# Two of four weight sums of a hybrid decoder layer, made by adding DMA transfers instead of VectorE

## The chip, the cores and the metric

The kernel runs on one core of one Trainium2 chip. A core has five engines with a queue of instructions each: TensorE (PE: matmuls, PEld: its weight loads), VectorE (DVE), ScalarE (ACT), GpSimd (POOL) and SyncE (SP). SP only issues transfers here, POOL issues some too. Transfers are carried out by 16 DMA engines. An engine takes its own instructions strictly in order, and engines wait for each other through semaphores.

The metric is the device time of one execution in microseconds, the median of several runs. One further execution is profiled; its span, from the first to the last instruction, is a little shorter than the time of a run.

## The reference, cut to what matters

One layer on x of 512 tokens by 1024 features, all in fp32: a SwiGLU feed-forward network (FFN 1, hidden width 2816), then a mixer that merges windowed attention with a gated linear recurrence, then a second SwiGLU (FFN 2), each with a norm before and after.

```
def swiglu(x, w_gate, w_up, w_down):
    return (jax.nn.silu(x @ w_gate) * (x @ w_up)) @ w_down
...
f = swiglu(rms_norm(h, ffn1_norm_pre[l]), ffn1_w_gate[l], ffn1_w_up[l], ffn1_w_down[l])
h = h + 0.5 * rms_norm(f, ffn1_norm_post[l])
u = rms_norm(h, mix_norm_pre[l])
proj = u @ w_in[l]
q, k, v, xr, yr, gl = jnp.split(proj, splits, axis=-1)
...
gates = jax.nn.sigmoid(gl).reshape(B, S, N_BRANCHES, D_MODEL)
merged = gates[:, :, 0] * attn_d + gates[:, :, 1] * rec_d
h = h + rms_norm(merged @ w_out[l], mix_norm_post[l])
f = swiglu(rms_norm(h, ffn2_norm_pre[l]), ffn2_w_gate[l], ffn2_w_up[l], ffn2_w_down[l])
h = h + 0.5 * rms_norm(f, ffn2_norm_post[l])
```

What matters for the change are the products of x with blocks of weights: `w_gate` and `w_up`, the q and k columns of `w_in`, and half of its gate columns `gl`. Attention has twelve heads in three groups; one head of each group is merged with the other two into one output head, so there are four rounds, each of three q and three k blocks.

## The kernel before, in words

**Exactness.** Every fp32 operand of a matmul is split into a high part of reduced precision (ACT, L266) and the rest (DVE, L267). A product is then three matmuls: high by high, high by low, low by high.

**The weight stream.** All weights lie in one DRAM array in the order of their use, in groups of up to 1 MB (128 rows by 2048 numbers). `raw_of` (L204 to L222) loads the next group into one of two buffers `raw` by a transfer on SP (L212). A buffer is free for the next load when the last reader of its weights is through.

**Seven-product pairs.** A pair is two blocks of 1024 by 128 weights, called u and g (for FFN up and gate, for attention k and q). Each is cut in two along the 1024 (`u0`, `u1`, `g0`, `g1`, each 128 rows by 512 numbers in `raw`), and the tokens are cut in two halves. Two by two by two blocks need eight products; by Winograd's form of Strassen's scheme seven are enough, for sums of weights and sums of tokens formed before. `w_forms` (L561 to L578) makes the weights for the seven products:

- `s12[:, 1] = u0 + u1` (L567), `s12[:, 0] = s12[:, 1] + g0` (L568), `u0 += g0` in place (L569), `g1 += s12[:, 0]` in place (L572): four adds on DVE of 128 by 512.
- Four splits: a from `g0`, `g1` as loaded (L571, for p1 and p2); b from `s12` (L573, for p6 and p5); c from `u0 + g0` and `u1` (L574, for p7 and p4); d from the new `g1` (L575, for p3).

`seven` (L580 to L619) runs the products in the order p1, p2, p6, p5, p7, p4, p3. Each is 12 matmuls of 256 columns (L591, L592, L593 in turn), 84 for a pair. Partial sums are copied out by ACT (L598) and added by DVE (L603).

There are 51 pairs: 17 in FFN 1 (hidden blocks 5 to 21), 16 in the mixer (twelve q and k pairs, named by block numbers such as (8,20), then four pairs of gate columns), and 18 in FFN 2. In the FFNs a "down" block, 48 matmuls of 512 columns against `w_down`, mostly follows every two pairs. In the mixer one round of attention (`attend`, L856 to L964) is written between the three pairs of the next round (`qk`, L835).

**Buffers.** Two of `raw`, two of `s12` (tag "s"), four of the large splits (a, b and c), two of d, five PSUM banks `acc` and three `aux`.

**The order.** A scheduler fixes the order of each engine's instructions when the program is built. Work is written in the order of the code; what stands under `tc.high_priority(offset=n)` is placed as if written n instructions earlier. `w_forms` stands under AHEAD = 100 and the evacuations of PSUM in `seven` under EVAC = 200. In the mixer `pair_of` (L828) makes the weight forms of the next pair ahead of the products of the present one, and the FFN's "prep" does the same.

**Attention's exchange.** `exchange` (L906 to L916) moves statistics across partitions: DVE masks them (L909), PE multiplies them by a constant matrix (L912), DVE masks and sums the result (L914, L916). It is called twice a round, and between the calls stand nine small operations (L919 to L931). PE takes L912 in its order among the products of the next round's pairs.

Of the kernel before, what the change touches and what calls it, by code (L numbers as in the profile page):

```python
# [13 lines left out]
ALU = mybir.AluOpType  # L14
AX = mybir.AxisListType

P = 128
# [136 lines left out]
def hybrid_layer(ctx: ExitStack, tc: tile.TileContext, xT: bass.AP, xN: bass.AP, wst: bass.AP,  # L154
                 first: bass.AP, rows: bass.AP, consts: bass.AP, bias: bass.AP, out: bass.AP):
    nc = tc.nc
    DVE, ACT, PE = nc.vector, nc.scalar, nc.tensor
# [44 lines left out]
    state = {"g": 0, "i": 0, "off": 0, "raw": None}  # L202

    def raw_of(key):  # L204

        g, i = state["g"], state["i"]
        grp = groups[g]
        if i == 0:
            w = grp[-1][1] + grp[-1][2]
            raw = wpool.tile([P, RAW_W], F32, name="raw", tag="raw", bufs=2)  # L210
            src = bass.AP(tensor=wst.tensor, offset=wst.offset + state["off"], ap=[[w, P], [1, w]])
            nc.sync.dma_start(raw[:, :w], src)  # L212
            state["raw"] = raw
            state["off"] += w * P
        k, o, w = grp[i]
        assert k == key, (k, key)
        src = state["raw"][:, o:o + w]
        if i + 1 == len(grp):
            state["g"], state["i"] = g + 1, 0
        else:  # L220
            state["i"] = i + 1
        return src  # L222

    def fetch(key, slot=None, ahead=0):

        with tc.high_priority(offset=ahead if slot else AHEAD):
            src = raw_of(key)
            w = src.shape[-1]
            t = slot() if slot else w8() if w > 512 else w4()
            split(t[:, 0, :w], t[:, 1, :w], src)  # L230
            return t[:, 0, :w], t[:, 1, :w]

    def w8():
        return wpool.tile([P, 2, 1024], F32R, name="w8", tag="w8", bufs=4)

    def w4():
        return wpool.tile([P, 2, 512], F32R, name="w4", tag="w4", bufs=2)
# [27 lines left out]
    def split(dh, dl, src):  # L265
        ACT.activation(dh, src, AF.Copy)  # L266
        DVE.tensor_sub(dl, src, dh.bitcast(F32))  # L267
# [293 lines left out]
    def w_forms(key):  # L561

        with tc.high_priority(offset=AHEAD):
            raw = raw_of(key)
            u0, u1, g0, g1 = (raw[:, i * 512:(i + 1) * 512] for i in range(4))
            s12 = spool[0].tile([P, 2, 512], F32, name="s12", tag="s", bufs=2)
            DVE.tensor_add(s12[:, 1, :], u0, u1)  # L567
            DVE.tensor_add(s12[:, 0, :], s12[:, 1, :], g0)  # L568
            DVE.tensor_add(u0, u0, g0)  # L569
            a, b, c, d = w8(), w8(), w8(), w4()  # L570
            split(a[:, 0, :], a[:, 1, :], raw[:, 1024:2048])  # L571
            DVE.tensor_add(g1, s12[:, 0, :], g1)  # L572
            split(b[:, 0, :], b[:, 1, :], s12.rearrange("p s c -> p (s c)"))  # L573
            split(c[:, 0, :], c[:, 1, :], raw[:, 0:1024])  # L574
            split(d[:, 0, :], d[:, 1, :], g1)  # L575
            lo, hi = slice(0, 512), slice(512, 1024)
            return {"p1": a[:, :, lo], "p2": a[:, :, hi], "p6": b[:, :, lo], "p5": b[:, :, hi],
                    "p7": c[:, :, lo], "p4": c[:, :, hi], "p3": d}  # L578
# [42 lines left out]
    def ffn(n, x, r, forms_x, apool, pss):  # L621
# [52 lines left out]
        for ev in ffn_order(n):  # L674
            if ev[0] == "std":
                j = ev[1]
                while len(pss) < 2 * j + 2:
                    pss.append(acc_ps())
                    gemm(pss[-1], fetch(keys[len(pss) - 1]), x)
                std_out(pss[2 * j], pss[2 * j + 1], j)  # L680
                if j < len(steps):
                    steps[j]()
            elif ev[0] == "prep":
                forms[ev[1]] = w_forms(("gu", n, ev[1]))
            elif ev[0] == "down":
                down(ev[1], ev[2])
            else:
                prod(ev[1], forms.pop(ev[1]), ev[2], ev[3])
# [4 lines left out]
    def act_two(pool):  # L693

        ts = [pool.tile([P, 8, T], F32R, name="act", tag="act", bufs=3) for _ in range(2)]
        return Act([ts[0][:, k, :] for k in range(8)], [ts[1][:, k, :] for k in range(8)])
# [22 lines left out]
    u1 = act_two(ap1)  # L719
# [9 lines left out]
    for k in range(KC):  # L729
        wh, wl, raw = wts[k]  # L730
# [30 lines left out]
    with ExitStack() as mx:  # L761
# [61 lines left out]
        pairs = [[(g * 4 + hd, 12 + g * 4 + hd) for g in range(NG)] for hd in range(NH)]  # L823
        order = [("pair",) + p for ps in pairs for p in ps] + [("pair", 52 + c, 53 + c) for c in range(0, KC, 2)]
        forms = {order[0]: w_forms(order[0])}
        steps[2]()

        def pair_of(key):  # L828

            i = order.index(key)  # L830
            if i + 1 < len(order):
                forms[order[i + 1]] = w_forms(order[i + 1])
            return forms.pop(key)
# [153 lines left out]
    with ExitStack() as mx:  # L987
# [10 lines left out]
        o, w = SMALL["ap"]  # L998
# [262 lines left out]
```

## Time and profile before

| | |
|---|---|
| runs (us) | 1249.63, 1248.39, 1248.76; median 1248.76 |
| span of the profiled execution | 1246.4 us |
| mean granted TensorE clock | 0.998 |
| PE busy | 1233.0 us, 99% of the span, 7712 matmuls |
| DVE busy | 913.5 us, 73%, 1447 instructions |
| ACT busy | 670.4 us, 54%, 1105 instructions |
| POOL busy | 26.2 us, 2%, 51 instructions |
| transfers | 141.37 MB, of it 122.86 MB by queues of hardware and 17.30 MB by those of software (POOL's) |

The profiled execution took 1246.4 us by its span; the median of the runs is 2.4 us above that.

How to read it: the page of the profile gives busy time by engine, a strip of 40 slices, the chain of waits that ended last, the costliest groups of instructions and the transfers by kind. L591 is line 591 of the kernel. A busy time of PE is not PE at its peak, since the ends of pipelined matmuls are modelled. A row of the timeline has its start in us from the start of the span, its length, the engine (SPq is SP's queue), the line, the operation, output and input, the shape, and how many instructions were merged into it. "us to landing" is the time from the issue of a transfer until its last byte is there.

### The profile page before, as it was taken

The page shows a single profiled execution, that of the slowest core. Times are in us where ns is not written, and L with a number is a line of the kernel's source. Part 1 is how long each engine was busy: PE and PEld are TensorE (multiplying, and loading weights), DVE is VectorE, ACT ScalarE, POOL GpSimd, SP SyncE. Part 2 cuts the span into 40 slices and gives each one's busy share as a digit, 9 for nine tenths or more (in the row PEclk, how much of TensorE's full clock was granted, in tenths as well). Part 3 has the DMA queues.
Part 4 walks back from the last instruction along what each step waited for, and adds up shares of the span by engine and source line. Part 5 has one row for each costly group of instructions (what it writes and reads, how often), then busy time and mean ns, then how long its engine had stood idle before and what let it go on. Part 6 is the DMA issues. An engine that isn't in the chain of part 4 may idle for free.

```text
span 1246.4 us, 18979 instructions
## 1 busy us (share of the span) xinstructions
PE 1233.0 (99%) x7712; PEld 1115.6 (90%) x7712; DVE 913.5 (73%) x1447; ACT 670.4 (54%) x1105; POOL 26.2 (2%) x51
## 2 busy tenths in 40 slices
PE   9999999999999999999999999999999999999997
PEld 8899999999878899999987787888899999999986
DVE  7996777786576588888565877664795867777755
ACT  7555444445355465666536979634564544445432
POOL 0000000000002000000000000000100000000000
PEclk9999999999999999999999999999999999999999
DMA  6222222235414222231342122224451322222241
GB/s 242 103 85 104 102 104 103 102 114 200 167 74 144 102 81 98 77 111 69 121 151 101 68 101 102 101 101 169 141 166 67 136 102 102 102 102 73 101 183 67
DMA packets 27383, 141.37 MB, mean 113 GB/s; under 512 B 2976, under 2 KB 6176, under 8 KB 13216
## 3 DMA queue, kind: packets, MB, share of 16 engines
q1 hardware_dynamic: 20016, 122.86, 27.4%
q0 software_dynamic: 7280, 17.30, 4.1%
q8 instruction: 60, 0.98, 0.3%
q14 instruction: 27, 0.22, 0.1%
HBM read 129.67 MB, written 6.29 MB: 109 GB/s over the span
## 4 chain that ended last, share of the span: by engine, by line
PE 89%; DVE 5%; ACT 4%; issue 1%; DMA 0%; SPq 0%; DVEq 0%; ACTq 0%
PE acc L591 11%; PE acc L592 11%; PE acc L593 11%; PE acc L385 7%; PE acc L387 7%; PE acc L386 7%; PE acc L281 7%; PE acc L280 6%; PE acc L279 6%; PE aux L592 3%; PE aux L591 3%; PE aux L593 3%; PE acc L790 1%; PE acc L792 1%; PE acc L791 1%
## 5 line engine op out<-in xcount | busy, mean ns | idle before, releaser
L267 DVE TENSOR_TENSOR w<-raw,w 128x1024 fp32r<-128x1024 f32 (+1 forms) x240 | 256.7, 1073 | 111.2 <-ACT w L266 79.4
L266 ACT ACTIVATE w<-raw 128x1024 fp32r<-128x1024 f32 (+1 forms) x240 | 224.5, 939 | 176.9 <-DVE raw L572 59.8
L591 PE MATMUL acc<-big,w 128*128 128x256 f32 x880 | 250.8, 285 | 0.0
L592 PE MATMUL acc<-big,w 128*128 128x256 f32 x880 | 249.9, 284 | 0.0
L593 PE MATMUL acc<-big,w 128*128 128x256 f32 x880 | 249.6, 284 | 0.0
L591 PEld LDWEIGHTS acc<-big,w 128*128 128x128 f32 x880 | 168.6, 192 | 0.9
L592 PEld LDWEIGHTS acc<-big,w 128*128 128x128 f32 x880 | 168.7, 192 | 0.6
L593 PEld LDWEIGHTS acc<-big,w 128*128 128x128 f32 x880 | 168.7, 192 | 0.0
L598 ACT ACTIVATE c<-acc 128x256 f32<-128x256 f32 x169 | 64.1, 379 | 80.0 <-PE acc L593 76.4
L386 PE MATMUL acc<-wd,act 128*128 128x512 f32 x256 | 99.8, 390 | 0.0
L385 PE MATMUL acc<-wd,act 128*128 128x512 f32 x256 | 99.6, 390 | 0.0
L387 PE MATMUL acc<-wd,act 128*128 128x512 f32 x256 | 99.4, 389 | 0.0
L591 PE MATMUL aux<-big,w 128*128 128x256 f32 x280 | 79.2, 283 | 0.0
L592 PE MATMUL aux<-big,w 128*128 128x256 f32 x280 | 79.2, 283 | 0.0
L593 PE MATMUL aux<-big,w 128*128 128x256 f32 x280 | 79.2, 283 | 0.0
L591 PE MATMUL acc<-tx,w 128*128 128x256 f32 x268 | 76.1, 284 | 0.0
L592 PE MATMUL acc<-tx,w 128*128 128x256 f32 x268 | 75.8, 283 | 0.0
L593 PE MATMUL acc<-tx,w 128*128 128x256 f32 x268 | 75.8, 283 | 0.0
L281 PE MATMUL acc<-big,w 128*128 128x512 f32 x192 | 74.7, 389 | 0.0
L280 PE MATMUL acc<-big,w 128*128 128x512 f32 x192 | 74.7, 389 | 0.0
L279 PE MATMUL acc<-big,w 128*128 128x512 f32 x192 | 74.7, 389 | 0.0
L267 DVE TENSOR_TENSOR w<-s,w 128x1024 fp32r<-128x1024 f32 x51 | 62.4, 1224 | 10.1 <-ACT w L266 10.1
(314 smaller groups left out, 2762.1 us busy)
## 6 DMA issues: line engine op xcount, KB each, us to landing
raw<-in_w SPq DMA_DIRECT2D x110, 1024.0 KB, 4.8
big<-act POOLq DMA_DIRECT2D x6, 512.0 KB, 3.3
gains<-in_rows POOLq DMA_DIRECT2D x5, 512.0 KB, 5.0
h<-in_x SPq DMA_DIRECT2D x8, 256.0 KB, 5.2
h<-in_xn POOLq DMA_DIRECT2D x4, 512.0 KB, 7.0
kept_m<-h POOLq DMA_DIRECT2D x4, 512.0 KB, 2.9
h<-kept_m POOLq DMA_DIRECT2D x4, 512.0 KB, 5.6
kept<-h POOLq DMA_DIRECT2D x4, 512.0 KB, 3.3
```

Source lines behind the costliest of these rows:

```text
L266: ACT.activation(dh, src, AF.Copy)
L267: DVE.tensor_sub(dl, src, dh.bitcast(F32))
L279: PE.matmul(ps, wh, xh, start=first, stop=False)
L280: PE.matmul(ps, wh, xl, start=False, stop=False)
L281: PE.matmul(ps, wl, xh, start=False, stop=last)
L385: PE.matmul(ps, x.hi[k][:, bl], wh, start=k == 0, stop=False)
L386: PE.matmul(ps, x.hi[k][:, bl], wl, start=False, stop=False)
L387: PE.matmul(ps, x.lo[k][:, bl], wh, start=False, stop=k == x.n - 1)
L591: PE.matmul(ps, wh, xh, start=start and k == 0, stop=False, skip_group_check=True)
L592: PE.matmul(ps, wh, xl, start=False, stop=False, skip_group_check=True)
L593: PE.matmul(ps, wl, xh, start=False, stop=k == 3, skip_group_check=True)
L598: ACT.activation(c, ps, AF.Copy)
```

## The change

Two of the four adds of `w_forms` are no longer on DVE. `u0 + u1` is formed by a transfer on SP that copies u0 from DRAM into `s12[:, 1]`, and a transfer on POOL that reads u1 from DRAM and adds it onto what lies there (`accum_op=ALU.add`). `u0 + g0` is formed by a transfer on POOL that reads g0 from DRAM and adds it onto u0 in `raw`, once the load of the group has landed. `raw_of` keeps the group's place and width in the stream, so that `stored(i)` can name the i-th 512 columns of it in DRAM. The adds of L568 and L572 and the four splits stay, with later line numbers (L575, L578, L577, L579, L580, L581); everything behind is 6 lines further on (L597, L598, L599 for the matmuls, L918 for the exchange).

```
             src = bass.AP(tensor=wst.tensor, offset=wst.offset + state["off"], ap=[[w, P], [1, w]])
             nc.sync.dma_start(raw[:, :w], src)
-            state["raw"] = raw
+            state["raw"], state["at"], state["w"] = raw, state["off"], w
             state["off"] += w * P
...
             u0, u1, g0, g1 = (raw[:, i * 512:(i + 1) * 512] for i in range(4))
+
+            def stored(i):
+                return bass.AP(tensor=wst.tensor, offset=wst.offset + state["at"] + i * 512,
+                               ap=[[state["w"], P], [1, 512]])
+
             s12 = spool[0].tile([P, 2, 512], F32, name="s12", tag="s", bufs=2)
-            DVE.tensor_add(s12[:, 1, :], u0, u1)
+            nc.sync.dma_start(s12[:, 1, :], stored(0))
+            nc.gpsimd.dma_start(s12[:, 1, :], stored(1), accum_op=ALU.add)
+            nc.gpsimd.dma_start(u0, stored(2), accum_op=ALU.add)
             DVE.tensor_add(s12[:, 0, :], s12[:, 1, :], g0)
-            DVE.tensor_add(u0, u0, g0)
             a, b, c, d = w8(), w8(), w8(), w4()
```

## The prediction

> **What bounds the kernel now.** I read the busy table and the chain of waits first, then a table by stage, then the instruction order of one stretch in the mixer, last the DMA rows.
>
> ```profile
> span 1246.4 us, 18979 instructions
> PE 1233.0 (99%) x7712; PEld 1115.6 (90%) x7712; DVE 913.5 (73%) x1447; ACT 670.4 (54%) x1105; POOL 26.2 (2%) x51
> ...
> PE 89%; DVE 5%; ACT 4%; issue 1%; DMA 0%; SPq 0%; DVEq 0%; ACTq 0%
> ```
>
> TensorE (PE) is busy for all but 1246.4 - 1233.0 = 13.4 us, so no change to VectorE (DVE) can win more than that. The 5% of DVE on the chain need a place, which the table by stage gives (columns: length; busy us and count of PE, PEld, DVE, ACT, POOL; clock; DMA share; GB/s).
>
> ```profile
> 407.00:456.00 49.00, 49.00 (x342) 46.00 (x341) 32.75 (x48) 22.69 (x34) 0.00 (x0) 1.00 0.27 96
> 456.00:495.00 39.00, 38.98 (x324) 38.59 (x323) 32.82 (x66) 23.78 (x55) 0.00 (x0) 1.00 0.25 85
> 670.00:712.00 42.00, 39.70 (x174) 32.23 (x173) 33.35 (x47) 35.77 (x46) 0.00 (x0) 1.00 0.24 89
> ```
>
> In the pairs of the mixer (first row) PE never pauses, and with attention among them (second row) for 0.02 us. The third row is the recurrence, where PE does lose 2.3 us; no pair is made there, so the change does not reach it. The sums of a pair are therefore hidden today, and the question is whether they stay hidden.
>
> **What is removed.** Two of four adds in each of 51 pairs (columns: count, busy us, mean ns of one, idle before):
>
> ```profile
> L568 DVE TENSOR_TENSOR s<-s,raw 128x512 f32<-128x512 f32 x51 | 34.9, 683 | 0.4
> L567 DVE TENSOR_TENSOR s<-raw 128x512 f32<-128x512 f32 x51 | 34.8, 683 | 0.3 <-DMA raw<-in_w 0.3
> L569 DVE TENSOR_TENSOR raw<-raw 128x512 f32<-128x512 f32 x51 | 34.8, 682 | 0.0
> ```
>
> L567 and L569 go: 34.8 + 34.8 = 69.6 us of DVE rows, 913.5 to about 844. On PE's path they are worth nothing. The one place where PE sits right behind DVE in this part is the second exchange of attention:
>
> ```profile
> 472.40 0.17 DVE L909 TENSOR_TENSOR xch<-e,cst 128x16 f32<-128x16 f32 x1
> ...
> 472.20 0.28 PE L592 MATMUL acc<-big,w 128*128 128x256 f32 x1
> 472.32 0.28 PE L593 MATMUL acc<-big,w 128*128 128x256 f32 x1
> 472.62 0.40 PE L912 MATMUL aux<-xch,cst 128*128 128x16 f32 x2
> ```
>
> PE issues a 256-column matmul every 0.12 us, so L912 could have gone at 472.44; it lost 0.18 us. Four heads make 0.7 us, the whole gain that I can find (0.06%). In the changed program's order the second L912 of each head stands 12 to 15 matmuls (at 0.12 us each, 1.4 to 1.8 us) earlier on PE, since the DVE queue ahead of it is shorter by about three adds of 0.6 us. That takes up what DVE gains there, so I count 0.
>
> **What is added, and when it can run.** Per pair: one 256 KB copy into s12 on SP, and two 256 KB adding transfers on POOL (one onto s12, one onto u0 in raw). 51 x 3 x 0.26 = 40 MB more to move. For the times I follow pairs (8,20) and (1,13), where pairs stand closest:
>
> ```profile
> 420.62 11.74 SPq L212 DMA_DIRECT2D raw<-in_w  x2
> ...
> 428.08 1.22 DVE L267 TENSOR_TENSOR w<-s,w 128x1024 fp32r<-128x1024 f32 x1
> ...
> 437.23 0.68 DVE L567 TENSOR_TENSOR s<-raw 128x512 f32<-128x512 f32 x1
> 437.83 1.22 DVE L267 TENSOR_TENSOR w<-s,w 128x1024 fp32r<-128x1024 f32 x1
> 438.96 0.68 DVE L568 TENSOR_TENSOR s<-s,raw 128x512 f32<-128x512 f32 x1
> ...
> 440.91 1.23 DVE L267 TENSOR_TENSOR w<-raw,w 128x1024 fp32r<-128x1024 f32 x1 [0.67 <-ACT w L266]
> ...
> 442.17 0.33 SPq L212 DMA_DIRECT2D raw<-in_w  x1
> ...
> 446.49 0.28 PE L591 MATMUL acc<-tx,w 128*128 128x256 f32 x1
> ...
> 449.37 0.28 PE L591 MATMUL acc<-big,w 128*128 128x256 f32 x1
> ```
>
> The loads of raw for (8,20) and (1,13) go out at 420.62 and 432.03 (the merged row's end less 0.33), that for (5,17) at 442.17, right when the split at 440.91 has released its buffer. A raw load lands 4.8 us after its issue (below), so (1,13) is there at 436.8 and L567 follows at 437.23. Behind it on DVE stands the split of s12 of (8,20), which ends at 439.05 and is first used at 446.49 (p6): 7.4 us in hand. The split of the two u sums of (8,20) ends at 442.14 and is used at 449.37 (p7): 7.2 us in hand.
>
> In the changed program's order the copy into s12 stands on SP ahead of the raw load of its own pair. It needs only a free s12 buffer, and there are two: for (1,13) that is the end of the split of (4,16), 428.08 + 1.22 = 429.30, when nothing is left to wait ahead of it on SP. The next load behind it goes at 432.03 anyway, so SP's queue loses nothing.
>
> The trace has no adding transfer, so I bound it by the nearest rows (KB each, median us to landing; then one POOL store alone):
>
> ```profile
> raw<-in_w SPq DMA_DIRECT2D x110, 1024.0 KB, 4.8
> big<-act POOLq DMA_DIRECT2D x6, 512.0 KB, 3.3
> kept_m<-h POOLq DMA_DIRECT2D x4, 512.0 KB, 2.9
> bs<-in_bias SPq DMA_DIRECT2D x4, 256.0 KB, 2.5
> ...
> 892.13 0.55 POOL L432 DMA_DIRECT2D kept<-h  x1
> ...
> DMA to landing us min/median/max: 8.0/8.0/8.0
> ...
> 892.21 0.33 SPq L212 DMA_DIRECT2D raw<-in_w  x1
> ```
>
> The copy is the same 128 rows of 2 KB as bs: 2.5 us, so 431.8. Call the adding transfer's time to landing X. Lower end 2.9 us: a POOL transfer of 512 KB on an idle queue, which is also what 256 KB cost if each byte is moved twice. Upper end 8.0 us: the store issued at 892.13, with a raw load issued 0.08 us behind it on SP. An adding transfer here is issued within 0.2 us of the load at 432.03, so the upper end is a likely case, not a freak. I take 6, nearer to it, because 256 KB are half of that store.
>
> A page of the Trainium skill, "Collectives: The Full Stack" (section on why ReduceScatter is half of AllGather), says that an adding transfer is slower because it reads two sources, not because the addition costs. By it an estimate for 256 KB is the 512 KB row, 2.9 us alone, the lower end; no run before this one shows it.
>
> With X = 2.9, 6 and 8 the sum in s12 is there at 434.7, 437.8 and 439.8. L575 (L568 today, at 438.96) also needs raw, 436.8. So the wait is over before, or 0.8 us after, the time of today. What it holds up is the split of s12 of (8,20) with 7.4 us in hand, then evacuations of p7 and p4, which are due only at the next pair but one (a pair takes three of the five acc banks). Cost on PE: 0.
>
> The u0 transfer waits for raw: (8,20) lands at 425.4, plus X at most 433.4, against its split at 440.91. 0 again; with its cover gone it would delay the next raw load one for one.
>
> On POOL, where an issue takes 0.55 us (the store's row), the two transfers of a pair stand one behind the other, so the s12 transfer of a pair queues behind the u0 transfer of the pair before, which waits for its own raw. For (1,13) that is over at 425.4, 6 us before it is wanted. POOL's other 47 transfers keep their places between the stretches with pairs and meet none of these.
>
> **FFN.** There a down block's 48 matmuls follow every two pairs, two raw loads go out together, and both copies into s12 leave before them, since their buffers are free one and two pairs earlier:
>
> ```profile
> 262.15 1.23 DVE L267 TENSOR_TENSOR w<-s,w 128x1024 fp32r<-128x1024 f32 x1
> ...
> 265.67 1.46 SPq L212 DMA_DIRECT2D raw<-in_w  x2
> ...
> 277.66 0.68 DVE L568 TENSOR_TENSOR s<-s,raw 128x512 f32<-128x512 f32 x1
> ```
>
> For the later pair the copy can go at 263.4, the sum is there at 263.4 + 2.5 + 8.0 = 273.9 at the worst, and is added to at 277.66. Hidden by 3.8 us.
>
> **Sum.** 1246.4 - 0 (adds) + 0 (copies, SP) + 0 (s12 transfers) + 0 (u0 transfers) = 1246.4 us of span. The median of the runs stands 2.4 us above this span, so 1249 us.
>
> **Rivals.**
>
> *Slower, because X is over 8.6: the ring of s12 sets the pace.* Split of s12, copy, adding transfer, L575, next split form a ring of 0.1 + 2.5 + X + 0.68 + 1.22 = 4.5 + X per pair. PE takes 84 x 0.12 = 10.1 us for a pair alone, and with attention among them a third of the time between these rows, 39.35 / 3 = 13.1 us:
>
> ```profile
> 510.92 0.25 PE L912 MATMUL aux<-xch,cst 128*128 128x16 f32 x1
> ...
> 550.27 0.37 PE L912 MATMUL aux<-xch,cst 128*128 128x16 f32 x2
> ```
>
> Up to X = 5.6 nothing drifts; up to 8.6 only pairs without a break do, and they are too few in a row (three, once five) to use up the 7.4 us in hand. At X = 10 the ring is 14.5: in the mixer 15 steps x 1.4 = 21 less the 7.4 in hand, 14 us; in FFN 2 the run of five, 4 x 4.4 - 7.4 = 10, and 1.4 each for two runs of three; 27 us together, 1276 us by the runs. Every further us of X costs 15 in the mixer alone. For it speaks that an addition in the transfer has no row at all, and that 8.0 has been seen for a plain store; against it, that this store was twice as large and waited for a load of 1 MB, and that the load is waited for here anyway.
>
> *Slower, in attention alone.* The whole softmax chain is one queue on DVE, and the add of the third pair (L575) stands between the two halves of the first exchange (after L909, ahead of L914). PE's L912 has been moved up to 1.8 us forward and has no work to jump to. If DVE doesn't reach the second exchange earlier, because it stands at L575 or waits for the split's ACT half, PE waits about 1.6 us in each of four heads, and as much again if the add is 2 us late: 4 to 13 us (1 to 3.2 us a head), 1253 to 1262, around 1257. For it: the 0.18 us above show that there is no slack. Against: three adds of 0.6 us do leave DVE's queue ahead of L912, and the s12 buffer for this add is free a pair ahead, as above.
>
> *Faster by more than 0.2%.* It needs 2.5 us from DVE's relief, and I find 0.7 (L912). The recurrence's 2.3 us of PE pauses are out of reach, since its DVE queue keeps its work. It would be 1246 at the lowest that the rows allow.
>
> **How the numbers follow.** No change: 0.44, at 1249. The ring: 0.24, from 1253 upwards with 1276 as its example, the highest third of it above 1285. Attention: 0.24, around 1257. Faster: 0.08. 0.2% of 1248.76 is 2.5 us, about what a measurement of this kernel can tell from no change. So faster 0.08, same 0.44, slower 0.24 + 0.24 = 0.48: slower is a little likelier than the same, but in two cases, each less likely than no change, so the time is that of no change, 1249, with a range of its own of 1247 to 1251. The full range reaches from 1246 (half of the faster case is left out) to 1284 (X of about 10.5; 0.1 left out above).
>
> **What the changed profile would show.** PE 1233 busy and a span near 1246; DVE about 844. The rows of the two adding transfers with 3 to 8 us to landing, the POOL issue about 0.55 us each, and L572's copy at 2.5 to 3. In the waits no row of L575 or of the second split waiting for POOL's transfers with more than some 20 us over 51 pairs, and none of PE behind them. Raw loads at the same spacing as before (11.4 and 10.1 us in the mixer's first pairs). The ring would show as DVE's L575 waiting for the transfer in every pair of the mixer, raw loads over 14 us apart and PE's share down in 407 to 620. Attention alone would show as idle time of PE before L912 (L918 in the new numbering). A landing of more than 8.6 us makes the forecast wrong; so does a raw load that lands much later than 4.8 us because the adding transfers share its DMA engines.

## The result and the profile after

The changed kernel took 1271.03 us (median of four runs, 1267.68 to 1272.72), the kernel before 1248.60 beside it: 22.4 us more, a ratio of 1.0172 with a 95% interval of 1.0156 to 1.0188. The profiled execution is the fastest of the four, with a span of 1265.7 us, 19.3 above that of before. First the busy table, the chain that ended last and the transfers of the page.

```profile
span 1265.7 us, 19345 instructions
PE 1238.4 (98%) x7712; PEld 1118.0 (88%) x7712; DVE 856.6 (68%) x1345; ACT 670.2 (53%) x1105; POOL 114.8 (9%) x153
...
PE 76%; DVE 9%; ACT 7%; DMA 6%; issue 2%; SPq 0%; DVEq 0%; POOL 0%; POOLq 0%; ACTq 0%
...
raw<-in_w SPq DMA_DIRECT2D x110, 1024.0 KB, 5.2
raw<-in_w POOLq DMA_DIRECT2D x51, 256.0 KB, 3.8
s<-in_w SPq DMA_DIRECT2D x51, 256.0 KB, 3.0
s<-in_w POOLq DMA_DIRECT2D x51, 256.0 KB, 6.2
```

DVE is relieved as foreseen (102 instructions fewer). The chain, which held no transfers before, has 6% of DMA now. The adding transfer onto s12 takes 6.2 us to landing in the median, near the 6 that the prediction took. The one onto u0, issued when raw has landed and mostly with no load of raw in flight, takes 3.8.

Where the time went shows best in how late the same matmul comes in each kernel. The table gives the start of the first matmul of a pair, less its start in the profile of before, in us; one profiled execution each. The kernels to the right of "changed" are the experiments below. A step from one row to the next is a loss between these two places.

| first matmul of | changed | s_only | plain | runs_dma | three_s8 | behind | behind_two |
|---|---|---|---|---|---|---|---|
| FFN 1, block 5 | +1.2 | +5.0 | +1.0 | +1.0 | +1.7 | +0.9 | +0.6 |
| FFN 1, block 9 | +4.6 | +6.7 | +3.3 | +3.5 | +2.9 | +2.7 | +1.2 |
| FFN 1, block 18 | +4.6 | +6.8 | +3.4 | +3.6 | +2.9 | +2.7 | +1.3 |
| FFN 1, block 19 | +6.9 | +7.1 | +3.4 | +3.6 | +3.1 | +4.7 | +1.3 |
| mixer, first pair | +6.9 | +7.1 | +3.4 | +3.6 | +3.0 | +4.9 | +1.3 |
| mixer, last pair | +7.3 | +9.7 | +4.5 | +3.6 | +9.5 | +5.5 | +1.8 |
| FFN 2, block 4 | +17.1 | +18.1 | +7.0 | +12.4 | +9.8 | +5.7 | +1.8 |
| FFN 2, block 10 | +19.5 | +19.6 | +8.2 | +15.2 | +14.4 | +7.1 | +2.8 |
| last matmul | +19.5 | +22.2 | +8.2 | +15.5 | +14.2 | +7.1 | +3.6 |

In the changed kernel the mixer, with its 16 pairs, loses 0.4 us. The regular stretches (blocks 9 to 18 of FFN 1, and FFN 2 from block 10 on) lose nothing. The loss sits at the start of FFN 1 (4.6), behind its block 18 (2.3), at the start of FFN 2 (9.8), and in the pairs that follow there (2.4). The largest loss comes from one place. The chain of waits of the changed kernel there reads (start, length, what):

```profile
936.50 4.69 DMA raw<-in_w
...
941.90 0.53 POOL raw L574
...
943.04 8.25 DMA s<-in_w
...
951.37 0.06 DVE s L575
...
951.98 0.70 DVE u L648
...
952.70 0.64 ACT act L266
...
953.38 0.79 PE acc L385
```

And the timeline of the same place, with the idle time ahead of each in brackets:

```profile
936.50 0.33 SPq L212 DMA_DIRECT2D raw<-in_w  x1
...
938.12 1.22 DVE L267 TENSOR_TENSOR w<-s,w 128x1024 fp32r<-128x1024 f32 x1
...
939.37 2.11 SPq L572 DMA_DIRECT2D s<-in_w  x2
...
941.89 0.85 POOL L574 DMA_DIRECT2D raw<-in_w  x1 [12.79 <-DMA raw<-in_w]
942.24 0.33 SPq L212 DMA_DIRECT2D raw<-in_w  x1
943.04 0.86 POOL L573 DMA_DIRECT2D s<-in_w  x1 [0.29 <-issue]
...
951.37 0.69 DVE L575 TENSOR_TENSOR s<-s,raw 128x512 f32<-128x512 f32 x1 [9.15 <-DMA s<-in_w]
951.98 0.69 DVE L648 TENSOR_TENSOR u<-acc,g 128x512 f32<-128x512 f32 x1
...
952.70 0.63 ACT L266 ACTIVATE act<-u 128x512 fp32r<-128x512 f32 x1 [7.33 <-DVE u L648]
...
953.38 0.79 PE L385 MATMUL acc<-wd,act 128*128 128x512 f32 x1 [7.07 <-ACT act L266]
```

L575 is the add of s12 for block 5 of FFN 2. Its copy into s12 leaves on SP at 939.37, right when the split at 938.12 has given the buffer back (938.12 + 1.22 = 939.34). Its adding transfer stands on POOL behind the u0 transfer, which waits for raw (landed at 941.2), and is in flight with a raw load issued at 942.24: 8.25 us. DVE waits 9.15 us for it. Behind it on DVE stands L648, which belongs to other work: the last plain block of FFN 2, whose `act` the down block (L385) needs. PE's matmuls for that block are done by 944.3 and DVE could have taken L648 then; it takes it at 951.98, and PE stands for 7.07 us.

In the kernel before, the same two instructions stand in the same order on DVE (L568 for L575, L642 for L648):

```profile
931.31 0.69 DVE L568 TENSOR_TENSOR s<-s,raw 128x512 f32<-128x512 f32 x1
...
936.67 0.69 DVE L642 TENSOR_TENSOR u<-acc,g 128x512 f32<-128x512 f32 x1 [2.94 <-PE acc L281]
```

There the sum is made 5.4 us ahead of the multiply, so the order costs nothing. The order is not new; the late sum makes it cost something.

The difference to see is that between the DVE rows at 951.37 and 951.98: the row with the long bracket isn't what PE needs next, the one behind it without a bracket is.

The pause has a second price. The windows around it show it (length, busy us and count of PE, PEld, DVE, ACT, POOL; clock; DMA share; GB/s):

```profile
944.00:946.30 2.30, 2.30 (x11) 1.57 (x9) 0.00 (x0) 1.06 (x1) 0.85 (x1) 1.00 0.88 297
...
953.30:955.00 1.70, 1.62 (x4) 1.33 (x5) 1.70 (x4) 0.03 (x1) 0.00 (x0) 0.50 0.31 57
955.00:957.00 2.00, 2.00 (x7) 1.52 (x6) 0.60 (x1) 0.66 (x2) 0.00 (x0) 0.50 0.00 0
957.00:958.50 1.50, 1.50 (x6) 1.22 (x5) 0.69 (x1) 0.46 (x1) 0.00 (x0) 0.64 0.00 0
958.50:960.00 1.50, 1.50 (x8) 1.23 (x7) 0.00 (x0) 0.60 (x1) 0.00 (x0) 1.00 0.00 0
```

After the pause TensorE is granted half its clock until about 958.1, with PE busy nearly throughout: (3.7 x 0.50) + (1.5 x 0.36) = 2.4 us more. 7.1 + 2.4 are the 9.8 us of the table but for 0.3.

### The profile page after: what moved, and what is told of

Its sections match the earlier page's. It is cut to its first block, busy times and chain, and to the rows that moved or that the text cites. A ratio compares the mean times of both kernels' runs of the same rounds, so it can differ in the third digit from the quotient of the medians.

```text
span 1265.7 us, 19345 instructions
## 1 busy us (share of the span) xinstructions
PE 1238.4 (98%) x7712; PEld 1118.0 (88%) x7712; DVE 856.6 (68%) x1345; ACT 670.2 (53%) x1105; POOL 114.8 (9%) x153
## 3 DMA queue, kind: packets, MB, share of 16 engines
q0 software_dynamic: 21968, 44.05, 16.5%
## 4 chain that ended last, share of the span: by engine, by line
PE 76%; DVE 9%; ACT 7%; DMA 6%; issue 2%; SPq 0%; DVEq 0%; POOL 0%; POOLq 0%; ACTq 0%
PE acc L597 10%; PE acc L598 10%; PE acc L599 10%; PE acc L385 6%; PE acc L386 6%; PE acc L387 6%; PE acc L280 4%; PE acc L279 4%; PE acc L281 4%; DMA raw<-in_w 3%; DMA s<-in_w 3%; PE aux L598 2%; PE aux L597 2%; PE aux L599 2%; DVE w L267 2%
## 5 line engine op out<-in xcount | busy, mean ns | idle before, releaser
L597 PE MATMUL acc<-big,w 128*128 128x256 f32 x880 | 250.6, 285 | 3.8 <-ACT c L604 3.8
L598 PE MATMUL acc<-big,w 128*128 128x256 f32 x880 | 249.6, 284 | 0.0
L599 PE MATMUL acc<-big,w 128*128 128x256 f32 x880 | 249.3, 283 | 0.0
L597 PEld LDWEIGHTS acc<-big,w 128*128 128x128 f32 x880 | 168.6, 192 | 5.4 <-ACT c L604 4.6
L598 PEld LDWEIGHTS acc<-big,w 128*128 128x128 f32 x880 | 168.8, 192 | 0.6
L599 PEld LDWEIGHTS acc<-big,w 128*128 128x128 f32 x880 | 168.7, 192 | 0.0
L604 ACT ACTIVATE c<-acc 128x256 f32<-128x256 f32 x169 | 64.0, 379 | 92.9 <-PE acc L599 88.9
L385 PE MATMUL acc<-wd,act 128*128 128x512 f32 x256 | 101.0, 395 | 7.9 <-ACT act L266 7.9
L597 PE MATMUL aux<-big,w 128*128 128x256 f32 x280 | 79.2, 283 | 0.0
L598 PE MATMUL aux<-big,w 128*128 128x256 f32 x280 | 79.2, 283 | 0.0
L599 PE MATMUL aux<-big,w 128*128 128x256 f32 x280 | 79.2, 283 | 0.0
L597 PE MATMUL acc<-tx,w 128*128 128x256 f32 x268 | 76.7, 286 | 2.5 <-ACT c L604 2.4
L573 POOL DMA_DIRECT2D s<-in_w x51 | 44.4, 870 | 383.1 <-DVE u L609 138.2
L599 PE MATMUL acc<-tx,w 128*128 128x256 f32 x268 | 76.4, 285 | 0.0
L598 PE MATMUL acc<-tx,w 128*128 128x256 f32 x268 | 75.9, 283 | 0.0
L279 PE MATMUL acc<-big,w 128*128 128x512 f32 x192 | 74.7, 389 | 0.0
```

The lines of the kernel that those rows point to most:

```text
L279: PE.matmul(ps, wh, xh, start=first, stop=False)
L385: PE.matmul(ps, x.hi[k][:, bl], wh, start=k == 0, stop=False)
L597: PE.matmul(ps, wh, xh, start=start and k == 0, stop=False, skip_group_check=True)
L598: PE.matmul(ps, wh, xl, start=False, stop=False, skip_group_check=True)
L599: PE.matmul(ps, wl, xh, start=False, stop=k == 3, skip_group_check=True)
L604: ACT.activation(c, ps, AF.Copy)
```

## The experiments

The theory (A): the chain of copy, adding transfer and add onto s12 comes too late where pairs follow the plain blocks or each other. Its sharper form, which came only with the last but one experiment, says that PE doesn't wait for that sum but for other work that stands behind L575 on DVE. Against A stood that the traffic as such slows the raw loads (B), that the u0 transfer is to blame (C), that every pair costs its share (D), and that something else than the buffers starts the chain late (E).

### One sum each

`u_only` puts u0 + u1 back on DVE, `s_only` puts u0 + g0 back.

```
u_only:
-            nc.sync.dma_start(s12[:, 1, :], stored(0))
-            nc.gpsimd.dma_start(s12[:, 1, :], stored(1), accum_op=ALU.add)
+            DVE.tensor_add(s12[:, 1, :], u0, u1)
s_only:
-            nc.gpsimd.dma_start(u0, stored(2), accum_op=ALU.add)
             DVE.tensor_add(s12[:, 0, :], s12[:, 1, :], g0)
+            DVE.tensor_add(u0, u0, g0)
```

> u0 + g0 stays with the adding transfer on POOL, u0 + u1 is an add on DVE again (no copy on SP, no adding transfer onto s12). Theory A, the chain copy, adding transfer, add on DVE of s12 holds up the pairs that follow each other without a down block: that chain is gone, so 1248 to 1251 us, PE gaps in 60 to 110 and 940 to 965 gone. Rival B, the added traffic slows the raw loads: a third of the traffic is left, about 1256. Rival C, the u0 transfer keeps raw and POOL's queue busy: all of the loss stays, 1266 or more.

> The other half: s12 by copy and adding transfer, u0 + g0 an add on DVE again. Theory A: nearly all of the loss, 1266 to 1272. Rival B: two thirds of it, about 1263. Rival C: 1249 to 1252.

Measured: u_only 1249.48 us, ratio 1.0005 (0.9996 to 1.0014), no difference; s_only 1270.52, ratio 1.0173 (1.0156 to 1.0190), all of the loss. The u0 transfer is free by itself, as the prediction had it, and C falls. B falls as the main cause: with a third of the traffic nothing is lost, and with two thirds all of it. In s_only the places differ a little: its loss at the start of FFN 1 is a pause of PE of 2.7 us with 3.4 us at a granted clock of 0.50 behind it. The groups of DVE's add of s12 show the wait (count, busy, mean ns, idle ahead of it and its releasers), u_only first:

```profile
L574 DVE TENSOR_TENSOR s<-s,raw 128x512 f32<-128x512 f32 x51 | 35.0, 686 | 0.7
```

then s_only:

```profile
L574 DVE TENSOR_TENSOR s<-s,raw 128x512 f32<-128x512 f32 x51 | 35.1, 687 | 43.2 <-DMA s<-in_w 34.1 <-DMA raw<-in_w 9.0
```

and the changed kernel, where the prediction had said that more than some 20 us here would speak against it:

```profile
L575 DVE TENSOR_TENSOR s<-s,raw 128x512 f32<-128x512 f32 x51 | 35.1, 689 | 52.5 <-DMA s<-in_w 40.4 <-DMA raw<-in_w 12.0
```

### What the addition in the transfer costs, and what the relief of DVE is worth

`plain` copies where the changed kernel adds, and `copy_only` leaves the two transfers of POOL out. Neither forms the sums, so they tell of times alone.

```
plain:
-            nc.gpsimd.dma_start(s12[:, 1, :], stored(1), accum_op=ALU.add)
-            nc.gpsimd.dma_start(u0, stored(2), accum_op=ALU.add)
+            nc.gpsimd.dma_start(s12[:, 1, :], stored(1))
+            nc.gpsimd.dma_start(u0, stored(2))
copy_only:
-            nc.gpsimd.dma_start(s12[:, 1, :], stored(1), accum_op=ALU.add)
-            nc.gpsimd.dma_start(u0, stored(2), accum_op=ALU.add)
```

> The changed kernel with plain copies in the place of the two adding transfers, so that s12 holds u1 alone and u0 is replaced by g0; same bytes to the same places, same order. If adding is what makes these transfers slow, the s12 transfer falls from 6.2 us to about 3 and by theory A most of the loss goes with it, 1250 to 1256. If a POOL transfer of 256 KB beside a raw load takes as long without the addition, 1266 to 1272 stays.

> The changed kernel without the two adding transfers: s12 gets u0 by the SP copy alone, u0 in raw stays as loaded; neither sum is formed. Theory A: a chain of 3 us is covered everywhere, 1247 to 1250, and since DVE is relieved of both adds this is also all that the relief can give: at most 0.7 us under the kernel before. Rival B: a third of the traffic, about 1256.

Measured: plain 1254.87 us, ratio 1.0045 (1.0030 to 1.0060); copy_only 1249.24, ratio 1.0005 (0.9995 to 1.0014). So both sums off DVE with nothing but a copy in their place win nothing: the ceiling of the change is no gain at all. Of plain, the queue row and the transfers:

```profile
q0 software_dynamic: 15440, 44.05, 10.3%
...
raw<-in_w POOLq DMA_DIRECT2D x51, 256.0 KB, 3.3
...
s<-in_w POOLq DMA_DIRECT2D x51, 256.0 KB, 5.0
```

and the queue row of the changed kernel:

```profile
q0 software_dynamic: 21968, 44.05, 16.5%
```

The same 44.05 MB need 6528 packets more with the addition, 64 for each of the 102 transfers. The time of POOL's queue on the 16 DMA engines goes up from 10.3% to 16.5%; less the 4.1% of before, that is 6.2% against 12.4%: an adding transfer keeps the DMA engines busy for twice as long. Onto u0, mostly alone, it lands only 0.5 us later (3.8 against 3.3); onto s12, mostly beside raw loads, 1.2 us later (6.2 against 5.0). Without the addition the time falls by 16 us all the same: at the start of FFN 2 PE pauses for 2.1 us in the place of 7.1 and keeps its clock, and in FFN 1 half of the loss is gone.

### Which pairs

`runs_dve` makes twelve pairs on DVE, `runs_dma` makes these twelve alone by transfers.

```
+            on_dve = key[0] == "gu" and key[2] in ((5, 6, 7, 8, 18, 19) if key[1] == 1 else (4, 5, 6, 7, 8, 9))
...
```

> Twelve pairs take their two sums on DVE as before, the other 39 by transfers: DVE for blocks 5 to 8, 18 and 19 of FFN 1 and 4 to 9 of FFN 2, where pairs follow the plain blocks or each other without a down block. Theory A, the loss sits in these places (4.6 + 2.2 + 9.7 + 2.1 us of the 19.5 by which the last matmul is late): 1249 to 1253 us. Rival D, every pair with transfers costs the same: 39/51 of 22 us are left, 1266 us.

> The reverse: transfers for these twelve pairs alone, DVE for the other 39. Theory A: nearly all of the loss, 1265 to 1272 us. Rival D: 12/51 of it, 1254 us.

Measured: runs_dve 1250.79 us, ratio 1.0014 (1.0004 to 1.0023); runs_dma 1262.50, ratio 1.0106 (1.0089 to 1.0123). D falls with both: 39 pairs cost 1.9 us, twelve cost 13.6. The two don't add up to 22.4; runs_dma was expected at 1265 or more. The table shows part of what is missing at the start of FFN 1 (3.5 in the place of 4.6), at block 18 (no loss there) and at the start of FFN 2 (8.8 in the place of 9.8). It can't show all of it: the two profiled executions are 4.3 us apart (1267.68 and 1263.36), the medians 8.5. Block 18's loss needs the transfers of block 20 too, as the last experiment shows.

### The buffers of s12

A third buffer under tag "s" needs room, which one of the two w4 buffers gives. The sums of tokens use the same tag and are changed alike.

```
three_s:
-            s12 = spool[0].tile([P, 2, 512], F32, name="s12", tag="s", bufs=2)
+            s12 = spool[0].tile([P, 2, 512], F32, name="s12", tag="s", bufs=3)
-        return wpool.tile([P, 2, 512], F32R, name="w4", tag="w4", bufs=2)
+        return wpool.tile([P, 2, 512], F32R, name="w4", tag="w4", bufs=1)
...
three_s8, besides (two_s8: this and w4, with two s buffers):
-            t = slot() if slot else w8() if w > 512 else w4()
+            t = slot() if slot else w8()
```

> The changed kernel with three buffers under tag s in the place of two; for the room, one buffer of the small splits (tag w4, used by p3) in the place of two. Theory A, the ring of two s12 buffers makes copy and adding transfer start late: they start a pair earlier, 1249 to 1256 us. Rival E, the buffers are not what starts them late (raw loads, queues, shared DMA engines): 1265 to 1272 us, as for two buffers; the single w4 buffer may add to both.

> Control for the next: the changed kernel with two buffers under tag s, one w4 buffer, and the 512-wide weights of the attention branch in w8 buffers. Both theories: as the changed kernel, 1266 to 1273 us, with 7 us of PE idle at the start of FFN 2.

> The same with three buffers under tag s. The first form with three lost 9 to 10 us in the attention branch, whose 512-wide weights had one w4 buffer left; that is gone here. Theory A (ring of two s12 buffers): 1251 to 1256 us, no idle stretch of PE at the start of FFN 2. Rival E: 1264 to 1272 us.

Measured: three_s 1264.83 us, ratio 1.0127 (1.0112 to 1.0142). Its profile had no pause at the start of FFN 2, but eight waits of PE of 0.7 to 1.8 us in the attention branch (L279, weights of 512 columns), where the single w4 buffer binds; that made the test unclear. With this mended, the control two_s8 took 1271.10, ratio 1.0173 (1.0156 to 1.0190), and three_s8 1256.42, ratio 1.0062 (1.0040 to 1.0084), with a wide spread of runs, 1252.06 to 1262.46. The third buffer takes two thirds of the loss away, against E. With the rows at 938.12 and 939.37 above, which show the copy waiting for its buffer, this says that two buffers, shared with the sums of tokens, start the chain late. It is not a test of their number alone: with a third buffer the transfers on SP and POOL stand in another order too. The profiled execution of three_s8 is its longest (1262.46) and has a new wait of PE of 3.9 us in attention (L898, near 464), with 6.8 us at half the clock around and behind it; that is the step from +3.0 to +9.5 in its column. There, too, DVE stands at L575: it waits 5.2 us for a raw load until 458.19, and attention's operations are queued behind.

### What PE waits for

`behind` leaves every transfer and buffer as in the changed kernel, and the order on PE, POOL and SP. It orders one add per FFN behind the last instruction of the last plain block on DVE (`state["std"]`); on DVE and ACT a few neighbours change places with it.

```
+            if key[0] == "gu" and key[2] == NSTD[key[1]] + 1:
+                with tc.issue_after(state["std"]):
+                    DVE.tensor_add(s12[:, 0, :], s12[:, 1, :], g0)
+            else:
+                DVE.tensor_add(s12[:, 0, :], s12[:, 1, :], g0)
...
```

> The changed kernel; only the add of s12 of one pair in each FFN (block 6 of FFN 1, block 5 of FFN 2) is queued on DVE behind the last instruction of the last plain block, whose u and split stood behind it. No transfer and no buffer changes. Theory A in its sharper form, PE does not wait for that sum but for the plain block's instructions queued behind the waiting add: the pause of 7.1 us at the start of FFN 2 goes and with it the lower clock behind it (2.5 us), 1258 to 1264 us. Rival F, PE needs the late sum itself there: the pause stays, 1268 to 1273 us.

Measured: 1255.05 us, ratio 1.0048 (1.0031 to 1.0064): 16 us of the 22.4 are back, more than expected (the profiled executions differ by 12.4). The timeline of behind at the start of FFN 2:

```profile
942.42 0.69 DVE L652 TENSOR_TENSOR u<-acc,g 128x512 f32<-128x512 f32 x1 [0.35 <-PE acc L281]
...
944.59 0.68 DVE L267 TENSOR_TENSOR act<-u,act 128x512 fp32r<-128x512 f32 x1
951.41 0.69 DVE L577 TENSOR_TENSOR s<-s,raw 128x512 f32<-128x512 f32 x1 [6.13 <-DMA s<-in_w]
```

and its windows there, columns as above:

```profile
940.00:952.00 12.00, 12.00 (x54) 9.76 (x53) 5.18 (x6) 2.68 (x5) 3.44 (x4) 1.00 0.86 213
952.00:964.00 12.00, 11.76 (x93) 11.35 (x92) 6.08 (x10) 6.48 (x11) 0.88 (x1) 1.00 0.26 53
```

The sum comes at 951.41, as late as in the changed kernel, and DVE still waits 6.13 us for it; but PE is busy for all of the 12 us, and the clock stays at 1.00. So PE didn't need that sum yet. It needed what was queued behind it.

### The rest: a load slowed by the transfers

The two longest waits of PE that behind has and the kernel before has not are at 100 (1.6 us) and 268 (1.8). They make about half of the 7.1 us that its profile is late; the rest is in steps of less than 1 us. In the changed kernel the second wait stands at 270; its timeline:

```profile
259.15 0.33 SPq L572 DMA_DIRECT2D s<-in_w  x1
...
260.88 0.33 SPq L212 DMA_DIRECT2D raw<-in_w  x1
...
263.26 0.88 POOL L573 DMA_DIRECT2D s<-in_w  x1 [5.73 <-DMA s<-in_w]
...
268.89 1.06 ACT L266 ACTIVATE wd<-raw 128x1024 fp32r<-128x1024 f32 x1 [2.13 <-DMA raw<-in_w]
269.85 0.37 ACT L604 ACTIVATE c<-acc 128x256 f32<-128x256 f32 x1
...
270.27 0.39 PE L597 MATMUL acc<-big,w 128*128 128x256 f32 x1 [2.06 <-ACT c L604]
```

The load of the down weights (260.88) lies between the copy and the adding transfer of block 20 and takes 8.0 us; the same load took 4.8 in the kernel before. ACT waits for it at its split, the copy out of PSUM (L604) stands behind the split, and PE needs the bank. It is the same pattern on another engine. `behind_two` is `behind` without the transfers of the two pairs that are in flight at the two waits (blocks 9 and 20 of FFN 1):

```
+            on_dve = key[:2] == ("gu", 1) and key[2] in (9, 20)
...
```

> The last kernel, and besides the sums of two pairs of FFN 1 (blocks 9 and 20) on DVE as before. The copies and adding transfers of these two are in flight with the load of the down weights that PE waited for in 100.4 (1.7 us) and 268.1 (1.9 us) there: the load of 1 MB took 6.5 and 7.5 us in the place of 4.8, ACT stood at its split, and the copy out of PSUM was queued behind that split. Theory G, these transfers slow the load: both waits go, 1250.5 to 1252.5 us. Rival H, the late sums of the pairs before them are the cause: both waits stay, 1254 to 1256.5 us.

Measured: 1253.92 us, ratio 1.0044 (1.0027 to 1.0061), between the two expectations. In the profiled execution the two loads take 4.7 and 4.6 us (behind: 6.5 and 7.5) and both waits of PE are gone, for a span of 1250.2 (behind: 1253.3). But of the four runs two took 1252 and two 1256 us, and of the latter there is no trace; each ratio lies within the other's interval, so the runs don't tell the two kernels apart. The profile does show that the two waits come from the slowed loads. Which of copy and adding transfer slows them isn't separated. What the longer runs wait for is open.

## Why the prediction was right and wrong

The time of 1271 us lies in the range of 1246 to 1284, on its slower side, which had the larger chance (0.48). But the likeliest case, no change at 1249, didn't come, and neither slower case came as it was drawn.

- *The adds on DVE, worth nothing*: right, copy_only shows it (1.0005). The rows of 34.8 us overstate the relief of DVE: busy time went down by 913.5 - 856.6 = 56.9 us, not 69.6, because neighbouring rows overlap (an add of 0.68 us lets the next instruction start after 0.60).
- *Copy 2.5 us, X = 6, at most 8.0, at least 2.9*: the copy takes 3.0; X is 6.2 in the middle, 3.7 to 9.6 over the 51, so the upper end was too low. The issue on POOL takes 0.87 us, not 0.55. The Trainium skill's "Collectives: The Full Stack" (why ReduceScatter is half of AllGather) says that ReduceScatter is slower because its add needs two source reads; the doubled engine time above agrees with that, while the 2.9 us that the prediction estimated by it for a transfer alone was 3.6 at the least (u0).
- *The u0 transfers, 0*: right, u_only shows it.
- *The mixer, 0, raw loads 11.4 and 10.1 us apart*: right. The mixer lost 0.4 us, and the loads of those pairs are 11.4 and 10.6 apart. The ring of 4.5 + X was to decide from X = 8.6 on; in the mixer X was 3.7 to 7.4, and it did not.
- *Attention alone*: didn't come. No wait of more than 0.4 us stands ahead of the exchange's L918 in the changed kernel.
- *FFN, "hidden by 3.8 us", and with it "0 (s12 transfers)" in the sum*: this is the step that failed. It was worked out for the regular stretch, where a down block follows every two pairs, and there it holds. It was taken for all of the FFN. At the start of FFN 2 s12's buffer comes free at 939.34 and X is 8.25, so the sum that the kernel before made at 931.31 comes at 951.37. Of the work queued behind L575 on DVE the prediction named the split of s12 and the evacuations of p7 and p4; there it is the last plain block, with no 7.4 us in hand. Behind shows that this queueing makes 16 of the 22.4 us.
- *"A raw load that lands much later than 4.8 us because the adding transfers share its DMA engines"* was named as what would make the forecast wrong, and so was a landing of more than 8.6 us. Both came. In the changed kernel late raw loads (6.1 and 8.0 us) cost about 1 us at block 8 of FFN 1 and 2 us behind its block 18. X was over 8.6 for eight of the 51, all in the FFNs and none in the mixer, where the limit had been worked out.

So the time fell into the range that was drawn for a ring in the mixer, but another mechanism brought it there. That the range held is luck.

## What to carry to other kernels

Where a sum is moved to a slower path that is hidden on the average, look at the places where the schedule changes its rhythm, and ask there not when the sum is needed but what stands behind the instruction that waits for it, on each engine that takes its work in order. One instruction that waits 9 us for a sum that TensorE doesn't need yet can stop TensorE, and placing one such instruction per FFN elsewhere gave back about as much as a third buffer did (1255.05 and 1256.42 us). A change whose best case can be bounded (here by leaving the work out) should be bounded first.

## What the runs showed of the hardware

- After 7.1 us without a matmul, TensorE was granted half its clock for about 4.7 us of busy work, 2.4 us of loss on top of the pause. That agrees with the Trainium skill's "TensorE: Matmul & The Clock Gate" (the HAM clock gate), which puts the drop to half the clock behind an idle window of some 3.4 us. Shorter pauses do not go by such a limit here: behind 2.7 us in s_only (at 65) and behind 1.9 us in two_s8 (at 77) the granted clock was 0.50 and 0.51 for 3.4 us, while the pause of 2.1 us in plain showed no drop (1.00 in the 5 us behind it). What decides between these isn't shown.
- An addition in a transfer of 256 KB costs little time to landing when it is mostly alone (3.8 against 3.3 us) and doubles the time that it holds the DMA engines (12.4% of the span against 6.2% for the 102 transfers).
